# Stores of the gated forms split and moved to SyncE's queue, stores of the output projection moved to ScalarE's

## The chip, the cores and the metric

The kernel runs on one core of a Trainium2 chip. Its time is the device time of one execution, in microseconds. A core has five engines that each run their own list of instructions in order: TensorE (PE, matrix products), VectorE (DVE), ScalarE (ACT), GpSimd (POOL) and SyncE (SP). SP here only issues DMAs. ACT and POOL issue DMAs too, between their computing instructions. In the profile "SPq" and "ACTq" mark what an engine's sequencer does (issuing a DMA) while its datapath is free.

## The reference

One transformer block on 512 tokens, model width 2048, in float32:

```
u = rmsnorm(x);  z, xbc, dt, q, k.., v.., gates = split(u @ w_in)
mixed = concat(ssd_mixer(...), nsa_mixer(...))
h = x + mixed @ w_out                       # output projection
v = rmsnorm(h)
h = h + (silu(v @ w_gate) * (v @ w_up)) @ w_down   # 2048 -> 5632 -> 2048
return rmsnorm(h)
```

The last two products with `w_gate` and `w_up` (2048 x 5632 each) and the one with `w_down` are more than half of the time.

## The kernel before

Every float32 product is split into float32r pieces. A value is stored as a high part (a rounded copy, made by ACT with `a_hi`, line 124) and a low part (value minus high part, made by DVE with `lo`, line 127). A product is then high x high + high x low + low x high. On top of that the feed-forward products use a Strassen form: a 256 x 256 block of weights (a "quad" of four 128 x 128 blocks 11, 12, 21, 22) is multiplied in seven products M1 to M7 in place of eight, on sums of weight blocks and sums of input halves.

The program runs in stages: input projection with the two mixers (to about 780 us), output projection (780 to 870 us), gate and up products (870 to 1710 us), down products (1710 us to the end).

**Output projection.** For each of 16 chunks `c` of 128 output rows, `ev_oa(c)` (line 1269) adds the residual, loaded from `h1_d` into one of four buffers, to the product in PSUM (DVE), stores the sum to `h_d` in memory (line 1273), and makes the scaled, split and combined forms that the gate and up products read: ACT lines 124, 1277 and 1280, DVE lines 127 and 136, POOL lines 1292 to 1295. `load_h1(c + 4)` (line 1267) then loads the next residual into the same buffer from SP's queue, which has to wait until the store has landed. In this stage a scheduler orders the instructions of the engines by a model of their times; in the stages behind it, the order is the order of the Python program.

**Gate and up.** There are 22 units `u` of 256 columns of `w_gate` (side 0) and `w_up` (side 1). A unit is 14 steps, one for each product and side, in the order M1, M5, M6, M2, M7, M3, M4. A step is 16 matmuls (eight blocks deep, a 512-column and a 256-column matmul each). Weights come in blocks of 512 KB in the order 11, S1, 12, S3, 22. S1 and S3 are sums of two blocks, and are made by DMA: SP loads one block (line 1158) and POOL issues a second, accumulating DMA onto it (line 1160) once the first has landed. ACT makes a block's high part three steps ahead of its use, DVE its low part two steps ahead. Results leave PSUM by ACT (lines 1426, 1428, 1436, 1438, 1449) and DVE (136). M6's result is copied out by line 1428 and M7 of the same side then reuses that PSUM bank, so PE can start M7 only when line 1428 is done. After side 1 the two sides are combined (lines 133, 1465, 1466) and a small task `g_forms(u)` (line 1471) computes the seven forms that the down products need, with high and low parts, into one tile `sg` of 128 x 7 x 512. Such tasks run beside the steps: `yield n` means "go on after n more ticks", and a step has 8 ticks. At the end `g_forms` stores all seven forms, 1792 KB, to `g_d[u]` in memory with one DMA from ACT's queue (line 1492). The next unit's `g_forms` writes the same tile `sg`.

**Down.** 35 visits multiply `w_down` with the forms, read back from `g_d`: the first five units' by ACT's queue (line 1580), the others by SP's (line 1598).

Loads are written into SP's list when the program's own allocation finds a free buffer (`advance`, line 1135); on the chip SP then waits until the engines have really released it, and everything behind in SP's list waits too. DMAs issued by SP and ACT also share eight completion counters in turn, and one is issued only after the DMA that had the same counter eight DMAs before has landed.

Of the kernel before, what the change touches and what calls it, by code (L numbers as in the profile page):

```python
# [17 lines left out]
NP = NFF // 2  # L18
# [96 lines left out]
def body(ctx, tc, xT, w_in, w_out, w_gate, w_up, w_down, w1k, w1v, cols, rows, kst, out):  # L115
    nc = tc.nc
# [3 lines left out]
    def f(ap):  # L120
        return ap.bitcast(F32)

    def a_hi(dst, src, scale=1.0):
        act.activation(dst, src, AF.Copy, scale=scale)  # L124

    def lo(eng, dst, src, hi):
        eng.tensor_tensor(dst, src, f(hi), ALU.subtract)  # L127

    def neg_lo(dst, src, hi):
        dve.scalar_tensor_tensor(dst, src, -1.0, f(hi), op0=ALU.mult, op1=ALU.subtract)  # L130
# [4 lines left out]
    def add(eng, o, a, b):  # L135
        eng.tensor_tensor(o, a, b, ALU.add)  # L136
# [17 lines left out]
    def ps_v():  # L154
        return ps("v", 1)
# [9 lines left out]
    h_d = dram.tile([NJ, 128, 4, 256], F32, name="h_d")  # L165
    g_d = dram.tile([NP, 7, 128, 512], F32, name="g_d")
# [105 lines left out]
    def col(c, n=1):  # L272
        return colc[:, c:c + n]
# [989 lines left out]
    def load_h1(c):  # L1263
        if c < KD:
            P2["h1", c] = (P2["HH"][:, 0:2].rearrange("p a t -> p (a t)"), P2["HH"][:, 2:4].rearrange("p a t -> p (a t)"),
                           P2["SR"].rearrange("p a t -> p (a t)"), rrow)[c % 4]
            (nc.scalar if c < 4 else nc.sync).dma_start(P2["h1", c], h1_d[c])

    def ev_oa(c):
        def ev(p):  # L1270
            h = P2.pop(("h1", c))
            add(dve, h, p, h)
            nc.gpsimd.dma_start(h_d[c // 2][:, 2 * (c % 2):2 * (c % 2) + 2, :].rearrange("p a t -> p (a t)"), h)
            t = P2["t", c % 2] = P2["TT"][:, 2 * (c % 2):2 * (c % 2) + 2].rearrange("p a t -> p (a t)")
            a_hi(t, h, scale=col(C_FN + c))
            if c == 0:
                act.activation(acc2, h, AF.Square)
            else:
                q = ps_v()
                act.activation(q, h, AF.Square)  # L1280
                add(dve, acc2, q, acc2)
            k = c // 2
            if c % 2 == 0:
                a_hi(P2["V0"][:, k, 0, :], t[:, 0:256])
                lo(dve, P2["V0"][:, k, 1, :], t[:, 0:256], P2["V0"][:, k, 0, :])
            else:
                e = P2["t", 0]
                vh, t2 = P2["VV"][:, :, k, 0, :], t.rearrange("p (a t) -> p a t", a=2)
                a_hi(vh, t2)
                lo(dve, P2["VV"][:, :, k, 1, :], t2, vh)  # L1290
                t1, t2 = P2["T1"][k // 4][:, k % 4, :], P2["T2"][:, k, :]
                pool.tensor_tensor(t1, e[:, 256:512], e[:, 0:256], ALU.subtract)
                pool.tensor_tensor(P2["T34"][:, 0, k, :], e[:, 256:512], t[:, 256:512], ALU.subtract)
                pool.tensor_tensor(t2, t1, t[:, 256:512], ALU.subtract)
                pool.tensor_tensor(P2["T34"][:, 1, k, :], t[:, 0:256], t2, ALU.add)
            load_h1(c + 4)
            sch.flags.add(("oa", c))
            if c == 7:
                sch.add(half_t())
        return ev  # L1300
# [14 lines left out]
    def half_t():  # L1315
        yield 12
        t_piece(0, 0)
        yield 16
        t_piece(1, 0)
# [89 lines left out]
    def gu_after(u, side, got):  # L1409
        both = u in (0, NP - 1)  # L1410

        def after(pr):
            def ev(p):
# [23 lines left out]
                elif pr == M5:  # L1437
                    act.activation(m5, p, AF.Copy)
                elif pr == M7:
                    add(dve, m5, p, m5)  # L1440
                elif pr == M3:
                    add(dve, u2, p, u2)
                    if both:
                        add(dve, c4[:, 1:4:2], wv[:, :, lo_h], wv[:, :, hi_h])
                elif pr == M4:
                    if both:
                        fold(c4[:, 2], p)
                    else:
                        act.activation(wv[:, 2, :], p, AF.Copy)
                        add(dve, c4, wv[:, :, lo_h], wv[:, :, hi_h])  # L1450
                    if side == 0:
                        rr = rrow[:, None, :].to_broadcast([128, 2, 512])
                        c2 = ct[:, 0]
                        mul(dve, c2, c2, rr)
                        sch.add(silu(u, g, c2, rr, 0 if both else 10))
                    else:
                        sch.run_until(("r", u))
                        mul(dve, c, c, g)
                        sch.add(g_forms(u))
# [11 lines left out]
    def g_forms(u):  # L1471

        ct = P2["CT"].rearrange("p (s c a) t -> p s c (a t)", s=2, c=2)
        g = ct[:, 1]
        tg = ct[:, 0].rearrange("p a t -> p (a t)").rearrange("p (a t) -> p a t", a=4)
        sg = P2["ST"][:, 0:14, :].bitcast(F32R).rearrange("p (v s) t -> p v s t", s=2)
        yield 10
        a_hi(sg[:, 0, 0, :], g[:, 0, lo_h])
        a_hi(sg[:, 1:3, 0, :], g[:, 1, :].rearrange("p (a t) -> p a t", a=2), scale=-1.0)
        gq = g.rearrange("p c (a t) -> p (c a) t", a=2)  # L1480
        dve.tensor_tensor(tg[:, 1, :], gq[:, 1, :], gq[:, 0, :], ALU.subtract)
        add(dve, tg[:, 2, :], gq[:, 1, :], gq[:, 3, :])
        add(dve, tg[:, 0, :], tg[:, 1, :], gq[:, 3, :])
        dve.tensor_tensor(tg[:, 3, :], tg[:, 0, :], gq[:, 2, :], ALU.subtract)
        yield 4
        lo(dve, sg[:, 0, 1, :], g[:, 0, lo_h], sg[:, 0, 0, :])
        neg_lo(sg[:, 1:3, 1, :], g[:, 1, :].rearrange("p (a t) -> p a t", a=2), sg[:, 1:3, 0, :])
        a_hi(sg[:, 3:7, 0, :], tg)
        yield 4
        lo(dve, sg[:, 3:7, 1, :], tg, sg[:, 3:7, 0, :])  # L1490
        yield 16
        nc.scalar.dma_start(g_d[u].rearrange("v p n -> p v n"), f(sg).rearrange("p v s t -> p v (s t)"))
        sch.flags.add(("g", u))

    PIECES = {1: (1, 1), 4: (2, 0), 5: (2, 1), 7: (3, 0), 9: (3, 1)}
# [114 lines left out]
    def g_rhs(p, lo_):  # L1610
        a = G_POS[V_OF[p]]
        return lambda k: (G[lo_ + k][:, a, 0, :], G[lo_ + k][:, a, 1, :])
# [155 lines left out]
    def down_before(v, n):  # L1768
        def before():
            if n == 1:  # L1770
                assert v < NJ - 2 or not any(fz.busy[NZ2:])
                add_h(v)
                if v:
                    P2["A2"] = P2["A"][:, 70:76, :]
            elif n == 0 and v == 27:
                x = GRING * 2 + 1
                assert max(i for i, y in enumerate(visits) if y[1] <= x < y[2]) < v
                close_pool("t0")
                P2["X"] = open_pool("t0", side="right").tile([128, 32, 128], F32, name="X")
            elif (v, n) == (0, 0):  # L1780
                close_pool("E")
                P2["E2"] = P2["E"] = open_pool("E").tile([128, NE, 128], F32, name="E2")
        return before
# [13 lines left out]
    for v, (j, a, b) in enumerate(visits):  # L1797
# [14 lines left out]
        for n, p in enumerate(SEQ_D):  # L1812
            blk, sums = q["form"][p]
            if n == 0 and v in (2, 3):
                later[5 + (v == 3)] = len(items)
            s = Step(blk, g_rhs(p, a), bk(p), after=af(p),
                     before=down_before(v, n) if n < 2 else None, sums=sums)
# [54 lines left out]
    with tc.manual_schedule(engines={mybir.EngineType.PE, mybir.EngineType.Activation, mybir.EngineType.DVE}):  # L1872
        for k in range(KD):
            if k % 4 == 0:
                issue_split(k // 4)
            t = xt[:, k, :]
# [113 lines left out]
```

## Time and profile before

| | us |
|---|---|
| three timed runs | 2210.35, 2211.69 (median), 2212.78 |
| the profiled execution, its own time | 2210.91 |
| its span, first to last instruction | 2209.1 |
| output projection, about | 780 to 870 |
| gate and up, about | 870 to 1710 |
| down, about | 1710 to 2209 |

The profile's page gives busy times per engine and groups of instructions. A row of the timeline is: start, duration, engine, line, operation, output<-inputs, shape, how many, and in brackets the idle time of the engine before it with what ended that. A row of the waits is: engine and line <- what it waited for: total us, times, longest. The chain of waits is followed back from the last instruction; a DMA in it stands with its start and the time until it landed. In the view of DMAs, q1 is SP's queue, q10 ACT's and q0 POOL's, with packets, MB and the share of the 16 DMA engines' time in the window.

### The profile page before, as it was taken

How to read it: one execution, taken by the hardware profiler on the slowest of the kernel's cores; microseconds unless marked ns; L12 is line 12 of the kernel's file. 1: busy time of each engine (PE TensorE's matmuls, PEld its weight loads, DVE VectorE, ACT ScalarE, POOL GpSimd, SP SyncE). 2: the span in 40 equal slices, each digit the busy share in tenths (PEclk: the TensorE clock that was granted, in tenths of full speed). 3: DMA queues.
4: the chain of work that ended last, by engine and by line, in shares of the span. 5: the costliest groups of instructions: out<-in, count | busy, mean ns of one | idle time of the engine just before them, and what ended most of it. 6: DMA issues, size and time to landing. Idle time of an engine off the chain costs nothing.

```text
span 2209.1 us, 35224 instructions
## 1 busy us (share of the span) xinstructions
PE 2151.5 (97%) x12924; PEld 1895.9 (86%) x12924; DVE 1779.7 (81%) x2791; ACT 1207.5 (55%) x2022; POOL 441.0 (20%) x460
## 2 busy tenths in 40 slices
PE   8999999999999999999999999999999999999997
PEld 6888888888788887888888888888888899999997
DVE  6799766878886658888888888888888888887896
ACT  5455456676676657555555555555555444343453
POOL 0002323424431135000000000000000232222232
PEclk9999999999999999999999999999999999999999
DMA  5222342223464467878888888788888879897974
GB/s 201 91 72 70 131 138 88 76 96 108 141 206 115 108 209 208 234 211 254 228 231 239 218 254 228 232 237 215 256 225 225 307 228 305 234 292 207 319 183 114
DMA packets 176141, 427.16 MB, mean 193 GB/s; under 512 B 18608, under 2 KB 25792, under 8 KB 175968
## 3 DMA queue, kind: packets, MB, share of 16 engines
q1 hardware_dynamic: 118592, 283.12, 38.1%
q0 software_dynamic: 30864, 90.09, 20.6%
q10 hardware_dynamic: 26512, 51.70, 6.5%
q8 instruction: 101, 1.65, 0.3%
q14 instruction: 72, 0.59, 0.1%
HBM read 358.78 MB, written 62.39 MB: 191 GB/s over the span
## 4 chain that ended last, share of the span: by engine, by line
PE 80%; DVE 8%; DMA 5%; ACT 4%; issue 3%; POOL 0%; DVEq 0%; SPq 0%; ACTq 0%; POOLq 0%
PE ps_s L1219 19%; PE ps_g L1219 10%; PE ps_g L234 7%; PE ps_g L236 7%; PE ps_g L235 7%; PE ps_t L1219 4%; PE ps_g L1225 2%; PE ps_g L1223 2%; PE ps_g L1224 2%; PE ps_t L1225 2%; PE ps_t L1223 2%; PE ps_t L1224 2%; PE ps_s L1223 2%; PE ps_s L1224 2%; PE ps_s L1225 2%
## 5 line engine op out<-in xcount | busy, mean ns | idle before, releaser
L124 ACT ACTIVATE R<-Z 128x1024 fp32r<-128x1024 f32 (+4 forms) x446 | 407.1, 925 | 418.5 <-DVE Z L136 299.8
L127 DVE TENSOR_TENSOR R<-Z,R 128x1024 fp32r<-128x1024 f32 (+4 forms) x355 | 376.5, 1068 | 28.6 <-ACT R L124 13.3
L234 PE MATMUL ps_g<-u,whi 128*128 128x512 f32 x778 | 320.9, 412 | 0.0
L236 PE MATMUL ps_g<-u,wlo 128*128 128x512 f32 x778 | 305.8, 393 | 0.0
L235 PE MATMUL ps_g<-u,whi 128*128 128x512 f32 x778 | 304.9, 392 | 0.0
L1219 PE MATMUL ps_s<-u,R 128*128 128x512 f32 (+1 forms) x1160 | 252.9, 348 | 8.2 <-ACT A L1428 8.1
L1219 PEld LDWEIGHTS ps_s<-u,R 128*128 128x128 f32 x1160 | 187.7, 188 | 39.7 <-ACT A L1428 13.1
L127 DVE TENSOR_TENSOR wlo<-wraw,whi 128x512 fp32r<-128x512 f32 x211 | 160.5, 762 | 60.9 <-ACT whi L124 59.7
L124 ACT ACTIVATE whi<-wraw 128x512 fp32r<-128x512 f32 x211 | 131.4, 624 | 109.7 <-PE ps_g L235 76.8
L236 PEld LDWEIGHTS ps_g<-u,wlo 128*128 128x128 f32 x778 | 146.1, 188 | 31.8
L234 PEld LDWEIGHTS ps_g<-u,whi 128*128 128x128 f32 x778 | 146.6, 188 | 23.5
L235 PEld LDWEIGHTS ps_g<-u,whi 128*128 128x128 f32 x778 | 147.0, 189 | 21.1
L1219 PE MATMUL ps_t<-u,R 128*128 128x512 f32 (+1 forms) x600 | 131.5, 348 | 0.0
L1219 PE MATMUL ps_g<-u,R 128*128 128x512 f32 x584 | 131.3, 349 | 0.0
L1219 PE MATMUL ps_s<-T,R 128*128 128x512 f32 (+1 forms) x560 | 125.7, 349 | 1.6 <-DVE R L127 1.6
L1219 PE MATMUL ps_g<-T,R 128*128 128x512 f32 (+1 forms) x584 | 126.0, 346 | 0.4 <-DVE R L127 0.4
L1219 PE MATMUL ps_s<-V,R 128*128 128x512 f32 (+1 forms) x568 | 123.8, 348 | 0.6 <-ACT V L124 0.3
L872 ACT ACTIVATE e<-e,em 128x128 f32<-128x128 f32 (+3 forms) x128 | 71.6, 559 | 78.8 <-DVE em L870 78.2
L127 DVE TENSOR_TENSOR E<-Z,R 128x1024 fp32r<-128x1024 f32 (+1 forms) x91 | 111.0, 1219 | 4.5 <-ACT R L124 4.1
L136 DVE TENSOR_TENSOR Z<-Z 128x1024 f32<-128x1024 f32 (+4 forms) x99 | 110.0, 1112 | 4.6 <-POOL Z L136 2.6
L1219 PEld LDWEIGHTS ps_t<-u,R 128*128 128x128 f32 x600 | 98.0, 188 | 14.0
L136 DVE TENSOR_TENSOR A<-ps_g,A 128x512 f32<-128x512 f32 (+1 forms) x102 | 67.3, 664 | 52.2 <-PE ps_g L1219 39.1
(507 smaller groups left out, 5623.5 us busy)
## 6 DMA issues: line engine op xcount, KB each, us to landing
Z<-in_w_up SPq DMA_DIRECT2D x94, 512.0 KB, 5.5
Z<-in_w_gate SPq DMA_DIRECT2D x94, 512.0 KB, 6.7
wraw<-in_w_in SPq DMA_DIRECT2D x164, 256.0 KB, 2.6
g_d<-A ACTq DMA_DIRECT2D x22, 1792.0 KB, 15.1
Z<-in_w_up POOLq DMA_DIRECT2D x37, 512.0 KB, 7.9
Z<-in_w_gate POOLq DMA_DIRECT2D x37, 512.0 KB, 7.2
u<-g_d SPq DMA_DIRECT2D x70, 256.0 KB, 5.5
Z<-in_w_down SPq DMA_DIRECT2D x55, 320.0 KB, 4.7
```

The lines of the kernel that those rows point to most:

```text
L124: act.activation(dst, src, AF.Copy, scale=scale)
L127: eng.tensor_tensor(dst, src, f(hi), ALU.subtract)
L136: eng.tensor_tensor(o, a, b, ALU.add)
L234: pe.matmul(p, hi_t[i][:, j, :], ah, start=(k == 0), stop=False)
L235: pe.matmul(p, hi_t[i][:, j, :], al, start=False, stop=False)
L236: pe.matmul(p, lo_t[i][:, j, :], ah, start=False, stop=(k == u.nk - 1))
L872: act.activation(e[:, 0:L], e[:, 0:L], AF.Exp, scale=-1.0, bias=m[:, 0:1], accum_out=m[:, 1:2])
L1219: pe.matmul(o, w, x, start=start, stop=(k == n - 1 and o is q), skip_group_check=not fresh[0])
L1223: pe.matmul(q, h[:, k, :], ah, start=(k == 0), stop=False)
L1224: pe.matmul(q, h[:, k, :], al, start=False, stop=False)
L1225: pe.matmul(q, l[:, k, :], ah, start=False, stop=(k == s.blk.n - 1))
```

## The change

Two places. In the output projection the 16 stores to `h_d` are issued by ACT in place of POOL. In `g_forms`, for all units but the last, the one store of seven forms from ACT's queue becomes seven stores of one form (256 KB) each from SP's queue, 8 ticks (one step) apart; the first is written 8 ticks after the last `lo` and the last 56 ticks after it, where the one store was written 16 ticks after. The last unit keeps its single store from ACT.

```diff
@@ ev_oa @@
             add(dve, h, p, h)
-            nc.gpsimd.dma_start(h_d[c // 2][:, 2 * (c % 2):2 * (c % 2) + 2, :].rearrange("p a t -> p (a t)"), h)
+            nc.scalar.dma_start(h_d[c // 2][:, 2 * (c % 2):2 * (c % 2) + 2, :].rearrange("p a t -> p (a t)"), h)
@@ g_forms @@
         lo(dve, sg[:, 3:7, 1, :], tg, sg[:, 3:7, 0, :])
-        yield 16
-        nc.scalar.dma_start(g_d[u].rearrange("v p n -> p v n"), f(sg).rearrange("p v s t -> p v (s t)"))
+        if u < NP - 1:
+            for v in range(7):
+                yield 8
+                nc.sync.dma_start(g_d[u, v], f(sg[:, v]).rearrange("p s t -> p (s t)"))
+        else:
+            yield 16
+            nc.scalar.dma_start(g_d[u].rearrange("v p n -> p v n"), f(sg).rearrange("p v s t -> p v (s t)"))
         sch.flags.add(("g", u))
```

How this moves instructions. First SP's list in the gate and up stage, from the gate loads of one unit to those of the next (the forms are in the tile that the list calls A; Z and A hold raw weight blocks). Before:

```order
L1158 DMA Z<-in_w_gate 128x1024 x4
L1158 DMA A<-in_w_gate 128x1024
L1158 DMA Z<-in_w_up 128x1024 x5
L1158 DMA Z<-in_w_gate 128x1024
L1158 DMA A<-in_w_gate 128x1024
```

and now:

```order
L1158 DMA Z<-in_w_gate 128x1024
L1494 DMA g_d<-A 128x512
L1158 DMA Z<-in_w_gate 128x1024
L1494 DMA g_d<-A 128x512 x2
L1158 DMA Z<-in_w_gate 128x1024
L1494 DMA g_d<-A 128x512 x3
L1158 DMA Z<-in_w_gate 128x1024
L1158 DMA A<-in_w_gate 128x1024
L1494 DMA g_d<-A 128x512
L1158 DMA Z<-in_w_up 128x1024 x5
L1158 DMA Z<-in_w_gate 128x1024
L1494 DMA g_d<-A 128x512
```

The seven stores stand between the five gate loads of a later unit, one, two, three and one of them, all behind the up loads whose sums POOL makes at that time. In ACT's list the store leaves; it stood behind the copies of M6 (line 1428) and M2 (line 1436) of side 0:

```order
L1438 ACTIVATE A<-ps_g 128x512
L124 ACTIVATE R<-Z 128x1024
L1428 ACTIVATE A<-ps_s 128x512
L124 ACTIVATE R<-Z 128x1024
L1436 ACTIVATE A<-ps_t 128x512
L124 ACTIVATE R<-Z 128x1024
L1492 DMA g_d<-A 128x7x512
L124 ACTIVATE R<-Z 128x1024 x2
```

Apart from that one row ACT's list is the same there. Last, POOL's list near the end of the output projection (rows 1292 to 1295 are its share of the combined forms, rows 1160 accumulating weight loads). Before:

```order
L1160 DMA Z<-in_w_up 128x1024
L1293 TENSOR_TENSOR A<-A 128x256
L1294 TENSOR_TENSOR A<-Z,A 128x256
L1160 DMA Z<-in_w_gate 128x1024
L1273 DMA h_d<-A 128x512
L1295 TENSOR_TENSOR A<-A 128x256
L1292 TENSOR_TENSOR Z<-A 128x256
L1273 DMA h_d<-rrow 128x512
L1273 DMA h_d<-A 128x512
```

and the same stores now, in ACT's list:

```order
L124 ACTIVATE R<-Z 128x1024
L1273 DMA h_d<-A 128x512
L124 ACTIVATE A<-A,colc 128x512
L124 ACTIVATE R<-A 128x1024
L124 ACTIVATE V_8575<-A 128x256
L1280 ACTIVATE ps_v<-A 128x512
L1273 DMA h_d<-rrow 128x512
L124 ACTIVATE A<-rrow,colc 128x512
L1273 DMA h_d<-A 128x512
```

The stores no longer stand behind POOL's accumulating loads; on ACT each stands just ahead of the scaling of the same chunk, which needs the same sum. A few neighbouring instructions of this stage change places on ACT, DVE and SP, because the scheduler's model sees other times.

## The prediction

> **What bounds the kernel now.** I read the busy time by stage first (us; busy us and count of PE, weight loads, DVE, ACT, POOL; clock; DMA share; GB/s), then what PE waited for in the gate and up stage, then the timeline around one such wait, then the DMAs behind it.
>
> ```profile
> 780.00:870.00 90.00, 84.62 (x383) 67.73 (x381) 60.56 (x82) 52.14 (x87) 47.03 (x59) 1.00 0.72 224
> 870.00:1710.00 840.00, 830.55 (x4745) 724.04 (x4746) 704.35 (x731) 473.74 (x621) 75.35 (x87) 1.00 0.82 231
> 1710.00:2209.10 499.10, 473.72 (x3880) 467.49 (x3878) 412.36 (x566) 211.12 (x331) 123.40 (x95) 0.98 0.82 243
> ```
>
> PE is the bound: in the gate and up stage it is idle for 840 - 830.55 = 9.5 us, in the output projection for 5.4 us. No edit here takes a matmul away, so all that can be won is idle time of PE in these two stages and at the turn to the third, some fifteen microseconds out of 2209. The question is which edit reaches which gap.
>
> ```profile
> PE ps_s L1219 <- ACT A L1428: 8.1, 12, 1.6
> ...
> ACT R L124 <- DMA Z<-in_w_up: 34.6, 19, 3.3
> ```
>
> The gaps of the gate and up stage are nearly all one wait: M7 waits for ACT's copy of M6 (line 1428), 12 times. ACT in turn waited 34.6 us for weight blocks of `w_up`, about once per unit. The timeline of one unit shows how the two hang together:
>
> ```profile
> 995.02 0.37 ACTq L1492 DMA_DIRECT2D g_d<-A  x1
> ...
> 996.61 0.86 POOL L1160 DMA_DIRECT2D Z<-in_w_up  x1 [9.88 <-DMA Z<-in_w_up]
> ...
> 1009.34 1.06 ACT L124 ACTIVATE R<-Z 128x1024 fp32r<-128x1024 f32 x1 [2.77 <-DMA Z<-in_w_up]
> ...
> 1011.35 0.58 ACT L1438 ACTIVATE A<-ps_g 128x512 f32<-128x512 f32 x1
> ...
> 1011.47 1.23 DVE L133 TENSOR_TENSOR A<-A,rrow 128x1024 f32<-128x1024 f32 x1 [2.81 <-ACT A L1466]
> ...
> 1013.93 1.06 ACT L124 ACTIVATE R<-A 128x1024 fp32r<-128x1024 f32 x1 [2.01 <-DVE A L136]
> 1014.90 0.58 ACT L1428 ACTIVATE A<-ps_s 128x512 f32<-128x512 f32 x1
> ...
> 1015.53 3.06 PE L1219 MATMUL ps_s<-u,R 128*128 128x512 f32 x16 [1.23 <-ACT A L1428]
> ```
>
> ```profile
> 992.78 3.30 DMA Z<-in_w_up
> 996.61 12.64 DMA Z<-in_w_up
> ```
>
> The store of seven forms is issued at 995.02. At 996.61 POOL issues the accumulating load that completes the block S3 of `w_up`; by the chain of waits it takes 12.64 us, to 1009.25. ACT stands idle from 1006.57 until then. Everything behind that block on ACT is late by 2.77 us, DVE waits for ACT (2.81), ACT for DVE (2.01), line 1428 ends late and PE loses 1.23 us. A shorter wait is absorbed; here is one that cost PE nothing:
>
> ```profile
> 1126.92 1.06 ACT L124 ACTIVATE R<-Z 128x1024 fp32r<-128x1024 f32 x1 [1.19 <-DMA Z<-in_w_up]
> ```
>
> So about 1.2 to 1.5 us of lateness is free, and the accumulating load has to land only some 1.6 us earlier (2.77 - 1.2) for this stall to go.
>
> **What the store does to that load.** The store's own rows for the stage, and the DMA queues while the store runs (995 to 1010) and in the other half of the same unit (1017 to 1027), when the sum S3 of `w_gate` is loaded in just the same way without a store beside it:
>
> ```profile
> L1492 ACTq DMA_DIRECT2D g_d<-A x21: 366/366/380, 915.7 to 1707.5; - x21
> DMA to landing us min/median/max: 14.6/15.1/16.9
> ```
>
> ```profile
> q1 hardware_dynamic: 636, 2.28, 42.8%
> q10 hardware_dynamic: 912, 1.84, 35.2%
> q0 software_dynamic: 144, 0.52, 17.5%
> ```
>
> ```profile
> q1 hardware_dynamic: 529, 1.93, 60.7%
> q0 software_dynamic: 144, 0.52, 27.7%
> ...
> Z<-in_w_gate POOLq DMA_DIRECT2D x1, 512.0 KB, 8.1
> ```
>
> With three queues at work the engines are 95% busy (42.8 + 35.2 + 17.5) and the accumulating load on q0 gets 17.5% of them; with two it gets 27.7% and lands in 8.1 us. The store takes about 15 us each time and always covers this load.
>
> **The change part by part.** *Seven stores on SP's queue.* In SP's new list one store follows the first of the five gate loads, two the second, three the third and one the last. What SP issues now, first all five gate loads and then the third alone:
>
> ```profile
> 996.15 19.22 SPq L1158 DMA_DIRECT2D Z<-in_w_gate  x5
> ...
> 1003.38 0.33 SPq L1158 DMA_DIRECT2D Z<-in_w_gate  x1
> ```
>
> So q10 is empty in the critical window, of the seven stores the first three run in it and three more from 1003 on, and they share SP's queue with the loads. I take the duration from the nearest row, the same load with two queues: 8.1 us, landing at 1004.7 in place of 1009.25. That is before ACT is free for it (1006.57): no wait, no stall. From the other side it cannot be worse than 12.64 unless the stores also delay the first load of S3, which is issued at 992.78, ahead of them.
>
> What it is worth: the matmuls of one product in three units that follow each other, in the chain of waits:
>
> ```profile
> 1077.83 2.78 PE ps_g L1219 x16
> ...
> 1116.76 2.78 PE ps_g L1219 x16
> ...
> 1155.72 2.78 PE ps_g L1219 x16
> ```
>
> Undisturbed units take 1116.76 - 1077.83 = 38.93 and 1155.72 - 1116.76 = 38.96 us. The 20 intervals between stores from 915.7 to 1707.5 take 791.8 us, 39.59 each, so 791.8 - 20 x 38.95 = 12.8 us are lost, of which the waits name 8.1. I take **-10 us**, between the two, since the small differences of units without a named wait may have other causes.
>
> The edit's price: ACT loses 21 issues of 0.37 us, worth nothing, as they stood behind line 1428 and 1436 and ACT is busy 474 of 840 us. SP gains 147 issues; by the same 0.37 us that is 54 us, hidden in SP's waiting for buffers:
>
> ```profile
> SPq L1158 <- DVE Z L136: 327.9, 40, 10.5
> ```
>
> Behind a store on SP stand weight loads. They queue up to three stores longer, 768 KB, which at the rate of the first window above (2.28 + 1.84 + 0.52 MB in 15 us, 309 GB/s) is 2.5 us. The block that this could make late is S3 of `w_gate`:
>
> ```profile
> 1017.91 0.86 POOL L1160 DMA_DIRECT2D Z<-in_w_gate  x1 [6.79 <-DMA Z<-in_w_gate]
> ...
> 1027.46 1.06 ACT L124 ACTIVATE R<-Z 128x1024 fp32r<-128x1024 f32 x1
> ```
>
> It lands at 1017.91 + 8.1 = 1026.0, 1.4 us before ACT turns to it, and another 1.2 are free. The three stores follow the load at 1003.38, ten microseconds ahead of S3's own, and are gone by then. I book 0, with 2.6 us of delay per unit as the point from which it costs.
>
> *Stores of the output projection on ACT.* POOL is rid of 16 issues, ACT gets them.
>
> ```profile
> 843.63 1.22 POOL L1273 DMA_DIRECT2D h_d<-A  x1
> ...
> 846.63 0.72 ACT L124 ACTIVATE A<-rrow,colc 128x512 f32<-128x512 f32 x1 [2.33 <-POOL A L1295]
> ...
> 851.09 0.50 PE L1223 MATMUL ps_g<-u,R 128*128 128x512 f32 x1 [2.36 <-DVE A L136]
> ...
> 857.27 0.69 DVE L136 TENSOR_TENSOR A<-ps_g,A 128x512 f32<-128x512 f32 x1 [1.31 <-DMA A<-h_d]
> ...
> 870.08 2.15 PE L1219 MATMUL ps_s<-T,R 128*128 128x256 f32 x11 [1.63 <-DVE R L127]
> ```
>
> ```profile
> 854.13 3.12 DMA A<-h_d
> ```
>
> The store at 843.63 stands on POOL behind two accumulating loads, and the reload of its buffer can start only at 854.13. DVE waits 1.31 us for that reload, and PE's 1.63 us at 870.08 lie in the same chain. PE's 2.36 us at 851.09 come through ACT, which waited 2.33 us for POOL's line 1295, itself behind the store's 1.22 us. On ACT the store can go some 3 us earlier and POOL's list is shorter by it. The most is 2.36 + 1.63 = 4.0 us of gain. The other end: 16 issues at 0.37 us all on the path cost 5.9 us; that would need ACT to be the bound, and it is busy 52 of 90 us and waits for the same sums anyway. I take **-2.5 us**: the 1.31 and half of the 2.33.
>
> *The turn to the down products.* The stores of unit 20 now stand between the first `w_down` loads, and ACT's queue, which loads the first units' forms there, is rid of 1.8 MB. PE loses this today:
>
> ```profile
> 1743.13 0.39 PE L1225 MATMUL ps_t<-V,R 128*128 128x256 f32 x1 [3.31 <-DVE R L127]
> ```
>
> The forms come earlier, the `w_down` loads later, with the same bytes: I book 0, with 3.3 us to either side.
>
> **Sum:** -10 - 2.5 = -12.5 us. From the profiled 2210.91 (span 2209.1 and 1.8 around it) that is 2198.4; the median of the runs is 0.8 higher, so **2199 us**.
>
> [...]
>
> **Rivals.**
> *The bytes decide, not the queues.* The engines are 95% busy while the store runs and as many bytes are waiting after the change; then the accumulating load still takes 11 to 12.6 us, the stalls stay, and only the 2.5 us of the output projection come: 2209. For it: that 95%. Against it: 8.1 us beside SP's queue alone at 88% (60.7 + 27.7). Chance 0.11. [...]
> *Half of it.* Stores of SP's queue slow the load to about 10 us in the worse units, or ACT pays for some of the 16 issues: half of 10 and 2.5, 2204 to 2206. Chance 0.11.
> *The stall at the turn goes too:* 3.3 more, 2196. Chance 0.10.
> *A new wait on the gate side.* SP's queue is served in order; if the stores make S3 of `w_gate` later than 2.6 us, every unit stalls in side 0. At 3.6 us it costs 1 us in 20 units: with the gain on side 1 kept, +20 - 12.5 = +7.5, 2219. For it: the margin is only 1.4 us before ACT waits. Against it: the stores are issued ten microseconds earlier. Chance 0.07.
>
> **How the numbers follow.** The forecast itself has 0.61 and alone would span 2195 to 2203. A change of under 0.2% (4.4 us) can't be told from none here. Faster is the forecast, the half and the larger gain, 0.82; the same is the first rival, 0.11; slower the last, 0.07. The range goes down to all 12.8 and half of the rest and up to the edge of the first rival: 2193 to 2208.
>
> **What would show it.** Right: ACT's wait for `in_w_up` falls from 34.6 us to under 8; the median accumulating load of `w_up` S3 lands in 8 to 9 us; PE's wait for line 1428 falls from 8.1 to under 2 us; units run at 38.95 us. The reload of 854.13 comes three or more microseconds earlier and PE's gap at 851 shrinks. Wrong: the load still takes over 11 us, or ACT waits for `in_w_gate`, or SP's loads show waits behind line 1494.

## The result and the profile after

The changed kernel takes 2197.39 us (median of 4 runs, 2193.58 to 2199.37), the kernel before in the same comparison 2211.02 (2208.35 to 2212.78). The ratio is 0.9936, 95% interval 0.9920 to 0.9952: faster by 10.6 to 17.7 us. Forecast were 2199 us, in a range of 2193 to 2208. The profiled execution took 2199.37 us, its span is 2197.6.

First the busy time of the gate and up stage of the changed kernel (start and end; length, then PE, weight loads, DVE, ACT and POOL in us with counts; granted clock, DMA share, GB/s), and the waits in it:

```profile
866.00:1695.00 829.00, 828.18 (x4752) 725.36 (x4752) 703.22 (x731) 476.85 (x620) 75.55 (x87) 1.00 0.83 234
```

```profile
PE ps_s L1219 <- ACT A L1428: 0.6, 1, 0.6
PEld ps_s L1219 <- ACT A L1428: 0.9, 1, 0.9
ACT R L124 <- DMA Z<-in_w_up: 3.3, 5, 1.2
```

PE is idle for 829.00 - 828.18 = 0.8 us in this stage, before it was 9.5. Its wait for line 1428 has gone from 8.1 us to 0.6, ACT's for blocks of `w_up` from 34.6 to 3.3. In the kernel before, PE's weight loads (PEld) waited for line 1428 longer and more often than its matmuls (870 to 1710 us):

```profile
PEld ps_s L1219 <- ACT A L1428: 13.1, 16, 1.9
```

So the stall showed at PE in 16 units, not only in the 12 of the row that the prediction used.

The timeline shows the place that was quoted of the kernel before, the block S3 of `w_up` of the same unit, and the same step of the next one:

```profile
992.04 0.86 POOL L1160 DMA_DIRECT2D Z<-in_w_up  x1 [10.38 <-DMA Z<-in_w_up]
...
1001.52 0.58 ACT L1426 ACTIVATE ps_t<-ps_s 128x512 f32<-128x512 f32 x1 [1.11 <-PE ps_s L1219]
1002.02 1.06 ACT L124 ACTIVATE R<-Z 128x1024 fp32r<-128x1024 f32 x1
...
1040.51 0.58 ACT L1426 ACTIVATE ps_t<-ps_s 128x512 f32<-128x512 f32 x1 [1.11 <-PE ps_s L1219]
```

ACT turns to the block without a wait, and the unit takes 1040.51 - 1001.52 = 38.99 us. The DMA queues during the accumulating load of that unit, first of the kernel before, then of the changed one (packets, MB, share of the 16 engines' time; below, the load with its us to landing):

```profile
q10 hardware_dynamic: 906, 1.83, 41.7%
q1 hardware_dynamic: 499, 1.81, 37.9%
q0 software_dynamic: 144, 0.52, 20.8%
...
Z<-in_w_up POOLq DMA_DIRECT2D x1, 512.0 KB, 12.6
```

```profile
q1 hardware_dynamic: 647, 1.85, 58.5%
q0 software_dynamic: 144, 0.52, 30.7%
...
Z<-in_w_up POOLq DMA_DIRECT2D x1, 512.0 KB, 9.4
```

ACT's queue (q10) is empty, POOL's (q0) has 30.7% of the engines in place of 20.8%, and its load takes 9.4 us in place of 12.6.

Two other places did less well: the output projection and the turn to the down products. They come below with their rows.

### The profile page after: what moved, and what is told of

It is laid out like the page before. It is cut to its first block, busy times and chain, and to the rows that moved or that the text cites. A ratio compares the mean times of both kernels' runs of the same rounds, so it can differ in the third digit from the quotient of the medians.

```text
span 2197.6 us, 35483 instructions
## 1 busy us (share of the span) xinstructions
PE 2151.6 (98%) x12924; PEld 1900.6 (86%) x12924; DVE 1777.5 (81%) x2791; ACT 1210.3 (55%) x2022; POOL 430.3 (20%) x444
## 5 line engine op out<-in xcount | busy, mean ns | idle before, releaser
L1219 PEld LDWEIGHTS ps_g<-T,R 128*128 128x128 f32 x584 | 96.3, 191 | 13.6
```

The costliest lines, as they stand in the source:

```text
L1219: pe.matmul(o, w, x, start=start, stop=(k == n - 1 and o is q), skip_group_check=not fresh[0])
```

## Experiments

In all traces PE has the same number of matmuls, 12,924, so the start of one and the same matmul can be compared. "Stretch" below is the time between the two matmuls that start at 915.3 and 1690.0 in the kernel before, about 19 and a half units of the gate and up products. "S3 load" is the accumulating load of S3 of `w_up`, median of the last 19 of them in the stretch, with the shortest and the longest; "wait" is the row of ACT for `Z<-in_w_up` from 870 to 1710 us, in which one wait for S1 of the last unit can be counted too (3.3 us before, 1.2 in the change, at most 5.4). All kernels are derived from the changed one.

| kernel | ratio to before, 95% interval | S3 load, us | wait, us | stretch, us |
|---|---|---|---|---|
| before | 1 | 11.56 (10.79 to 12.64) | 34.6 | 774.7 |
| the change | 0.9936 (0.9920 to 0.9952) | 9.71 (9.17 to 10.79) | 3.3 | 763.5 |
| the change again | 0.9946 (0.9927 to 0.9965) | 9.66 (8.97 to 10.18) | 4.1 | 763.5 |
| forms only | 0.9932 (0.9917 to 0.9948) | 9.86 (9.16 to 10.96) | 9.1 | 763.5 |
| output projection only | 0.9981 (0.9969 to 0.9993) | 11.54 (10.76 to 12.68) | 32.9 | 774.4 |
| one store on SP | 0.9928 (0.9912 to 0.9944) | 9.28 (8.52 to 10.61) | 5.3 | 763.6 |
| seven spread on ACT | 0.9923 (0.9908 to 0.9939) | 9.30 (8.66 to 10.18) | 6.3 | 763.8 |
| seven together on ACT | 0.9944 (0.9930 to 0.9959) | 10.26 (9.24 to 11.31) | 12.3 | 763.8 |
| one late on ACT | 0.9945 (0.9931 to 0.9959) | 9.29 (7.77 to 9.61) | 4.7 | 763.8 |
| extra store on ACT | 0.9997 (0.9986 to 1.0009) | 10.96 (10.34 to 12.40) | 32.0 | 770.9 |
| twice on SP | 1.0012 (1.0001 to 1.0022) | 9.12 (8.34 to 10.59) | 1.2 | 763.7 |
| unit 20 as before | 0.9938 (0.9924 to 0.9952) | 9.64 (9.15 to 10.01) | 2.5 | 763.5 |
| spread on ACT, unit 20 as before | 0.9926 (0.9913 to 0.9938) | 9.22 (8.83 to 10.28) | 7.3 | 763.5 |
| unit 20 as before, h_d on POOL | 0.9937 (0.9925 to 0.9950) | 9.41 (8.62 to 10.94) | 7.9 | 763.4 |

**Each half by itself.** The stores of the output projection back on POOL, the forms as changed:

```diff
-            nc.scalar.dma_start(h_d[c // 2]...
+            nc.gpsimd.dma_start(h_d[c // 2]...
```

> The stores of the forms split and on SP's queue, the stores of the output projection back on GpSimd. If the gain sits in the gate and up stage, as the trace of the change says (about -11 to -12.5 of its shifts), the time is 2198 to 2200 us. If the output projection gave the 2.5 us that the prediction booked, it is 2200 to 2202. If the two edits only work together, it is over 2204.

And the reverse, the stores on ACT and the forms as in the kernel before:

```diff
-        if u < NP - 1:
-            for v in range(7): ...
-        else: ...
+        yield 16
+        nc.scalar.dma_start(g_d[u]...)
```

> Only the output projection's stores on ScalarE; the forms stored by one DMA from ScalarE's queue as in the kernel before. The prediction's term: 2208.5 us (-2.5). The reading of the trace of the change: 2210 us (-0.9), because a new wait of TensorE for ScalarE (line 1280) and a spell of half clock take back what the earlier reload gives. ScalarE's wait for in_w_up stays at 30 us or more in both.

The forms alone give 0.9932, all of what the change gives, and the stretch falls by 11.2 us as in the change. The output projection alone leaves the stretch at 774.4 us and ACT's wait at 32.9. Its time is 0.9981, -4.2 us with an interval from -6.9 to -1.6 (a median of 2210.29 us against 2214.96 of the kernel before in that comparison); the prediction's -2.5 lies in it, the -0.9 of the trace does not. That value is taken up again below, since other comparisons do not show it.

**Queue or burst.** The one store of 1792 KB on SP's queue, without the split:

```diff
-            for v in range(7):
-                yield 8
-                nc.sync.dma_start(g_d[u, v], ...)
+            yield 16
+            nc.sync.dma_start(g_d[u]...)
```

> The change, but the seven forms of a unit stored by one DMA of 1792 KB on SP's queue, at the place where ScalarE issued it. Theory A, a third queue at work is what slows GpSimd's accumulating load: ScalarE's queue is still empty, the accumulating load of S3 of w_up takes 8 to 10 us, ScalarE's wait for in_w_up stays under 8 us, and the time is 2197 to 2201 unless the loads of w_gate behind the store get late. Theory B, it is the burst of 1.8 MB in the load's window, on whichever queue: the load takes 11 to 12.6 us, ScalarE waits 20 to 35 us and the time is 2205 to 2211. A third outcome, 1792 KB ahead of the gate loads on the same queue (some 6 us at 309 GB/s) make S3 of w_gate late: ScalarE waits for in_w_gate and the time is above 2212.

The split stores on ACT's queue:

```diff
-                nc.sync.dma_start(g_d[u, v], ...)
+                nc.scalar.dma_start(g_d[u, v], ...)
```

> The change, but its seven stores of one form each, 8 ticks apart, issued by ScalarE in place of SP. Theory A (the third queue): ScalarE's queue has work in the window of the accumulating load, which takes 11 to 12.6 us, ScalarE's wait for in_w_up stays at 20 us or more and the time is 2204 to 2210. Theory B (the burst): fewer bytes stand in the window, the load takes 9 to 10.8 us as in the change, the wait is under 8 us and the time 2196 to 2200, and issuing costs ScalarE 147 x 0.37 us that TensorE does not see.

Both have the whole gain (the load takes 9.28 and 9.30 us). So theory A (any third queue at work is enough) and theory B (the burst is enough, on whichever queue) each fall as they were put: a burst does this load no harm on SP's queue, and a third queue does none if its stores are spread. What both kernels lack is a burst on a queue of its own. The spread stores on ACT's queue also show that the gain doesn't come from sparing ACT the issues: it issues 147 stores there. The burst on SP's queue does leave a mark elsewhere: the accumulating load of S1 of `w_gate`, which comes next, takes 7.8 us in place of 5.4 (medians of 20), but the stretch shows no loss by it.

In the split form ACT's queue does have work beside the load, but only half as much:

```profile
q1 hardware_dynamic: 365, 1.30, 46.9%
q0 software_dynamic: 144, 0.52, 29.9%
q10 hardware_dynamic: 476, 0.88, 26.3%
...
Z<-in_w_up POOLq DMA_DIRECT2D x1, 512.0 KB, 8.8
```

The engines are fully busy here (46.9 + 29.9 + 26.3; the sum passes 100 because a packet counts where it starts), as in the kernel before, but ACT's queue, which is handed 256 KB at a time, takes 26.3% in place of 41.7% and leaves POOL's its 30%.

**Together, or later.** The seven stores on ACT's queue without the 8 ticks between them:

```diff
-            for v in range(7):
-                yield 8
-                nc.sync.dma_start(g_d[u, v], ...)
+            yield 16
+            for v in range(7):
+                nc.scalar.dma_start(g_d[u, v], ...)
```

> The seven stores of one form each on ScalarE's queue, without the 8 ticks between them: issued together where the one store stood. Theory A, a third queue that always has work (1.8 MB waiting) takes its share of the DMA engines from GpSimd's accumulating load: the load takes 11 to 12.6 us, ScalarE's wait for in_w_up is 25 to 35 us, the time 2206 to 2211 (the output projection's part kept). Theory B, small stores are served better than one large one: the load takes 9 to 10.8 us, the wait is under 10 us, the time 2196 to 2200.

The load takes 10.26 us, within theory B's 9 to 10.8 but longer than in the change. ACT's wait of 12.3 us lies between the two theories, and the stretch is 763.8: this much lateness is free. Nor do the stores go out together:

```profile
990.14 0.33 ACTq L1494 DMA_DIRECT2D g_d<-A  x1
...
990.98 4.90 ACTq L1494 DMA_DIRECT2D g_d<-A  x5
```

The last five take 4.9 us to be issued, about a microsecond each, so that less stands waiting when the load begins at 991.87. Why issuing is held up was not tried.

The one store 14 us later, beside the load of S3 of `w_gate`:

```diff
-            for v in range(7): ...
+            yield 56
+            nc.scalar.dma_start(g_d[u]...)
```

> One store of 1792 KB from ScalarE's queue as in the kernel before, but 56 ticks after the last low part in place of 16, 14 us later: it then runs from about 1009 to 1024 of a unit, beside most of the accumulating load of S3 of w_gate (1018 to 1026) and clear of that of w_up (997 to 1009). Theory A (a store on a third queue hurts whichever accumulating load it covers): the load of w_up takes 7.5 to 9.5 us and ScalarE's wait for in_w_up is under 6 us; the load of w_gate takes 10 to 12 us in place of 8.1, and with 1.4 us to spare ScalarE now waits 10 to 30 us for in_w_gate, of which 1.2 us a unit are free: the time is 2198 to 2205. Theory C (the up side is late for a reason of its own, the order of SP's or GpSimd's list): the wait for in_w_up stays at 20 us or more and the time is 2206 to 2211.

The disturbance moves with the store. The load of `w_up` falls to 9.29 us, and the load of S3 of `w_gate` rises to 10.41 (median of 19, 9.22 to 11.10) from 8.34 in the kernel before. ACT now waits for the other side, within what was expected:

```profile
ACT R L124 <- DMA Z<-in_w_gate: 15.1, 13, 6.9
ACT R L124 <- DMA Z<-in_w_up: 4.7, 2, 4.5
```

About 1 us per unit is too little to reach PE, and the stretch is 763.8 us. Theory C, that the up side is late by its own order, falls. This kernel also gives the length of the load of `w_up` with no store near it, 9.3 us.

**The same bytes on either queue.** A second store of the same seven forms to a scratch tensor `x_d` which nobody reads, once from ACT beside the change's stores, once from SP behind one undivided store (both with the output projection's stores on POOL):

```diff
             for v in range(7):
                 yield 8
                 nc.sync.dma_start(g_d[u, v], ...)
+                if v == 1:
+                    nc.scalar.dma_start(x_d[u]...)
```

> The change's stores of the forms (the output projection's back on GpSimd), and besides, per unit, one more store of the same seven forms, 1792 KB, from ScalarE's queue to a scratch tensor that nobody reads, at the place of the kernel before. Theory A (a third queue with much waiting takes its share of the DMA engines): the accumulating load of S3 of w_up rises from 9.7 us to 11.5 or more, ScalarE waits 30 us or more for in_w_up, the gate and up products (915 to 1690 in the kernel before) lose again what the change won there: 763.5 us becomes 775 or more. Theory D (what counts is the order and pace of SP's list, which stores in it thin out): the load stays at 9.3 to 10.3 us and the products at 763.5 to 765.

```diff
-            for v in range(7):
-                yield 8
-                nc.sync.dma_start(g_d[u, v], ...)
+            yield 16
+            nc.sync.dma_start(g_d[u]...)
+            nc.sync.dma_start(x_d[u]...)
```

> As many bytes as with the extra store, but all on SP's queue: one store of 1792 KB to the forms' place and one more of the same to a scratch tensor, directly behind it (the output projection's stores on GpSimd). Theory A (queues share, and bytes behind one another on a queue that is busy anyway do not add to its share): the accumulating load of w_up stays at 9 to 10 us. Theory E (waiting bytes count, on whichever queue): it rises to 11.5 us or more, as with the extra store on ScalarE's queue. In both the gate loads behind 3.6 MB come later, some 6 us at 309 GB/s, so that ScalarE may wait for in_w_gate and the time rise above 2210; what tells the theories apart is the load's duration.

The queues during the load of the same unit as above, first with the extra store on ACT's queue, then on SP's:

```profile
q10 hardware_dynamic: 909, 1.84, 44.3%
q1 hardware_dynamic: 512, 1.56, 35.3%
q0 software_dynamic: 144, 0.52, 22.1%
...
Z<-in_w_up POOLq DMA_DIRECT2D x1, 512.0 KB, 11.9
```

```profile
q1 hardware_dynamic: 489, 1.60, 57.0%
q0 software_dynamic: 144, 0.52, 35.8%
...
Z<-in_w_up POOLq DMA_DIRECT2D x1, 512.0 KB, 8.4
```

This pair decides between the theories. With 3.7 MB per unit to store in both, the load takes 10.96 us where half of them are on a third queue and 9.12 where all are on SP's; ACT's wait is 32.0 us against 1.2, the stretch 770.9 against 763.7. POOL's share is again about a fifth with three queues waiting and a third with two. Theory A was right on the cause and too high on the size (11.5 us or more, 775 or more): 7.5 of the 11.2 us are lost again. Theory E, waiting bytes on whichever queue, falls. That the stores on SP's queue are split in one kernel and not in the other makes little difference to this load, as the change and the one store on SP showed (9.71 and 9.28 us). Theory D, the pace of SP's list, falls too: with the extra store on ACT's queue that list is the one of the change, and the load is slow all the same. Neither kernel is faster than the one before, because both lose at the turn: the stretch behind this one, 1690 to 1760 in the kernel before, takes 79.4 and 83.4 us in place of 70.1. Unit 20's extra megabytes stand among the first loads of `w_down` there; that they alone do it was not tried.

**The turn and the output projection.** The change with unit 20 stored by one DMA from ACT, as unit 21 is:

```diff
-        if u < NP - 1:
+        if u < NP - 2:
```

> The change, but unit 20 too keeps its single store from ScalarE, as unit 21 does. If the 2 to 3 us that the trace of the change loses between 1724 and 1745 come from unit 20's seven stores standing between the first loads of w_down on SP's queue, TensorE's gaps at the turn sink from 5.1 us to the 4.9 of the kernel before but land later, no long spell of half clock follows, and the time is 2 us below the change's in this comparison. If they come from the stage ending 14 us earlier while the loads of w_down do not, the time is within 1 us of the change's.

> The change itself again, to stand beside the other three on one chip: 2197 us, within 2 us.

Two combinations of it, with the spread stores on ACT's queue, and with the stores of the output projection on POOL:

```diff
-        if u < NP - 1:
+        if u < NP - 2:
-                nc.sync.dma_start(g_d[u, v], ...)
+                nc.scalar.dma_start(g_d[u, v], ...)
```

> Seven spread stores on ScalarE's queue, unit 20 stored by one DMA as in the kernel before, the output projection's stores on ScalarE. The stretch of 915 to 1690 takes 763.5 us as in all spread forms; the turn (1690 to 1760) and the down products lose no more than 0.5 us against the kernel before where the change loses 3: 2195 to 2197 if TensorE's clock falls in no longer spell than before.

```diff
-        if u < NP - 1:
+        if u < NP - 2:
-            nc.scalar.dma_start(h_d[c // 2]...
+            nc.gpsimd.dma_start(h_d[c // 2]...
```

> The change with unit 20 stored as in the kernel before and the output projection's stores back on GpSimd. If the place of those stores is worth the 2.5 us of the prediction, it takes 2.5 us more than the same with them on ScalarE, in the time and in the stretch of 780 to 915; if it is worth under 1 us, the two agree within 1.5 us in the time and the stretch takes 133 to 135 us in both.

PE's two gaps at the turn, of the change and then of the kernel with unit 20 as before, each with the busy times of the microseconds after them, where the third number from the end is the granted clock (0.51, 0.57):

```profile
1725.48 0.58 PE L1225 MATMUL ps_t<-V,R 128*128 128x256 f32 x1 [3.34 <-DVE R L127]
1730.84 0.58 PE L1225 MATMUL ps_t<-V,R 128*128 128x256 f32 x1 [1.79 <-DVE R L127]
```

```profile
1724.00:1734.50 10.50, 7.24 (x32) 6.94 (x33) 10.30 (x15) 5.37 (x11) 3.21 (x2) 0.51 0.90 320
1734.50:1738.00 3.50, 3.50 (x31) 3.50 (x31) 3.50 (x4) 1.15 (x3) 1.57 (x1) 1.00 0.03 6
```

```profile
1723.84 0.39 PE L1225 MATMUL ps_t<-V,R 128*128 128x256 f32 x1 [1.54 <-DVE R L127]
1729.47 0.39 PE L1225 MATMUL ps_t<-V,R 128*128 128x256 f32 x1 [3.29 <-DVE R L127]
```

```profile
1730.00:1734.00 4.00, 4.00 (x23) 4.00 (x23) 3.97 (x9) 4.00 (x8) 0.00 (x0) 0.57 0.90 338
1734.00:1740.00 6.00, 6.00 (x53) 6.00 (x53) 5.90 (x7) 1.94 (x5) 4.37 (x2) 1.00 0.42 114
```

With unit 20 split on SP's queue the long gap comes first and PE's clock is halved for 10.2 us; with one store from ACT the gaps are those of the kernel before (1.54 and 3.31) and the clock is halved for 3.4 us. That is so in all three executions of the one form (the change, its repeat, forms only) and in all three of the other. One store of unit 20 on SP's queue does not do it either: its gaps are 1.79 and then 3.33 us, and the clock is halved for 3.4 us. The 70 us after the stretch take 71.2, 71.5 and 72.1 us in the first and 70.3, 70.0 and 71.1 in the second, against 70.1 in the kernel before. So unit 20's split on SP's queue costs about 1 us there, by the means of three. In the times it cannot be told: the medians are 2198.13 and, for the change again, 2199.91 us, the 2 us that were expected, but the ratios are 0.9938 and 0.9946 with intervals of 0.0014 and 0.0019 to either side. (The kernel before had 2212.70 in that comparison, so that the change's 2199.91, 2.9 above what was expected, is the same ratio within its interval.)

The kernel with spread stores on ACT and unit 20 as before has a median of 2196.75 us, 0.9926. That is the lowest median, but its interval overlaps the change's: not a version shown to be better.

For the output projection, the time from the matmul at 780.0 to the one at 915.3 of the kernel before, in each trace:

| its stores on | us | mean |
|---|---|---|
| POOL (before, forms only, extra store, twice on SP, unit 20 and POOL) | 135.3, 134.3, 133.7, 134.0, 132.0 | 133.9 |
| ACT (the other nine) | 133.1, 130.9, 135.2, 131.5, 134.1, 133.5, 134.9, 135.4, 133.6 | 133.6 |

The means differ by 0.3 us, each row scatters by 3 to 4.5. The pairs agree, each kernel against the one before in its own comparison: 0.9937 with the stores on POOL against 0.9938 on ACT, both with unit 20 as before, and 0.9932 against 0.9936 and 0.9946. The -4.2 us of the output projection alone is the one comparison that stands against this. Its profiled execution is also the quickest of the table, 130.9. It is one of three without a spell of half clock in that stretch, but the other two took 134.1 and 135.3. Whether the edit gives a microsecond or two stays open; next to the forms, nothing of it can be seen.

## Why the prediction was right, and where it was not

**The gate and up stage: right in cause, -11.2 us where -10 was booked.** The stretch went from 774.7 to between 763.4 and 763.8 us in every kernel that keeps the store from bursting on a third queue during the load, and back to 770.9 when a burst was added there again. "Units run at 38.95 us" came out as 38.99. The choice of 10 between 8.1 (named waits) and 12.8 (all intervals) was cautious: nearly all of the small differences belonged to the stall too. The row of the weight loads above, 13.1 us in 16 units, had named them.

**The mis-sized term: "I take the duration from the nearest row, the same load with two queues: 8.1 us".** The load of `w_up` took 9.71 us. That it is for the most part not the stores on SP's queue which lengthen it is seen from the late store: with no store near, it still took 9.29. The row of 8.1 was that of the other side of the unit, and that side's load is shorter. The prediction read the shares beside it, 60.7 and 27.7%, from a window of 10 us, longer than the load. In the load's own 8.1 us (1017.91 to 1026.0 in the kernel before) they are:

```profile
q1 hardware_dynamic: 382, 1.37, 55.6%
q0 software_dynamic: 144, 0.52, 34.2%
```

Beside the load of `w_up` without a store they are 60.4 and 28.1%. So these two queues keep the engines 90 and 89% busy, and SP's takes the larger part beside `w_up`; why it does is not shown by the runs. In the same way the prediction's 17.5% for three queues is of 15 us, and 20.8% in the load's own window. So "landing at 1004.7", well ahead of ACT, was too good: in the change the load lands 0.1 to 0.8 us before ACT turns to it, and in five units 0.2 to 0.9 us after. It was enough because 1.2 to 1.5 us are free, as the prediction had read from a wait of 1.19 us that cost PE nothing. Seven stores together on ACT come up to it (ACT waits for S3 in 14 units, at most 1.45 us, and 0.3 us of the stretch is lost), and the extra store goes over it.

**"The bytes decide, not the queues"** (0.11) fell by the pair of kernels with an equal number of bytes: which queue the store was on decided between 10.96 and 9.12 us for POOL's load. With three queues waiting in the kernel before, the shares were unequal (41.7, 37.9 and 20.8%).

**"A new wait on the gate side"** (0.07) did not come in the change. ACT's waits for `in_w_gate` are one of 2.9 us at the stage's start:

```profile
ACT R L124 <- DMA Z<-in_w_gate: 2.9, 1, 2.9
```

Its mechanism exists: the DMAs of SP's queue landed in the order of their issue (all 796 of the kernel before, all 943 of the change), and with 3.7 MB on that queue per unit ACT waits 18.8 us for `in_w_gate`, 16 times, and even that did not reach PE.

**The output projection: -2.5 us was booked, and 0.3 us with a scatter of 3 to 4.5 was found.** The steps happened, the sum did not. The reload that SP issued at 854.13 is issued at 843.79, and "three or more microseconds earlier" is right for its landing, but it now runs beside the weight loads and takes 10.0 us in place of 3.12. These are the issue on SP, what DVE waited for, and PE's gaps in the changed kernel:

```profile
843.79 0.32 SPq L1267 DMA_DIRECT2D A<-h_d  x1
```

```profile
853.84 0.69 DVE L136 TENSOR_TENSOR A<-ps_g,A 128x512 f32<-128x512 f32 x1 [1.53 <-DMA A<-h_d]
```

```profile
841.31 0.72 ACT L124 ACTIVATE A<-A,colc 128x512 f32<-128x512 f32 x1 [1.06 <-POOL A L1293]
843.19 0.58 ACT L1280 ACTIVATE ps_v<-A 128x512 f32<-128x512 f32 x1
```

```profile
843.87 0.47 PE L1223 MATMUL ps_g<-u,R 128*128 128x512 f32 x1 [1.46 <-ACT ps_v L1280]
...
863.07 1.05 PE L282 MATMUL ps_m<-ones,acc 128*128 128x1 f32 x8 [1.51 <-DVE acc L136]
```

DVE's wait for the reload is 1.53 us where it was 1.31. The gap of 2.36 at 851 is gone, and in its place PE waits 1.46 us, seven microseconds earlier, for line 1280, behind which again stands ACT's wait for POOL (line 1293 now, 1295 then). The prediction had taken a wait away and not asked what was late next.

**The turn: 0 with 3.3 us to either side.** About 1 us was lost in the 70 us after the stretch, by the order of the gaps and a longer spell of half clock (10.2 us in place of 3.4); all of 1690 to 2190 takes 503.0 us in the change against 500.0 before, but 504.3 also in a kernel whose turn is as before, so the rest is not ascribed to it. The rival by which this stall would go too (0.10) fell; so did "half of it" (0.11), whose slower load of some 10 us was there in the worse units but cost PE nothing.

In the profiled execution the parts are -0.7 (ahead of 780, where nothing was changed), -2.2, -11.2 and +3.0 us: -11.1 of the -11.5 between the two. The forecast of -12.5 was close in part by luck: a gain that cannot be seen in the output projection stood beside one too small in the gate and up stage.

## What to carry to other kernels

If a load on one queue is late by a microsecond or two, look at which other queues have much waiting just then, not only at how many bytes: move the burst to a queue that is busy anyway, spread it, or shift it to a time when the load has slack. Any of the three gave the whole gain here (a stretch of 763.6, 763.8 and 763.8 us in place of 774.7), because the stall only had to shrink below what the engines behind it absorb (an estimate of 1.2 to 1.5 us, from the wait of 1.19 us that cost PE nothing). Take a duration for the changed state from a row with the same neighbours, and shares from a window as long as the transfer; the same kind of transfer at another place in the loop was a microsecond off (8.1 us for `w_gate`, 9.29 for `w_up` with no store near).

## What the runs showed of the hardware that was not expected

The spells of half clock in the traces of the kernel before and of the change have two lengths: five last 3.41 us, and the one at the turn of the change lasts 10.24, three times as long (the last of each, which runs to the end, is left aside). Those at the turn stand at gaps of PE: one of 3.34 us followed by one of 1.79 (the change) cost 10.2 us of half clock, 1.79 followed by 3.33 (one store on SP) 3.4. But a gap of 2.36 us at 851 in the kernel before was followed by none, and one of 1.51 at 863 in the change by 3.4 us. Why like gaps end differently no run shows. What the traces show is that two gaps with an equal sum (5.13 and 5.12 us) need not cost the same.
